# Dilated attention on Trainium2: value projection of two head pairs at a time, with 512 weight columns for each strided stationary piece

## The chip, the cores and the metric

The kernel runs on one core of one Trainium2 chip. The metric is the device time of one execution in microseconds, and the median of the runs is compared. Five engines work beside each other: TensorE (PE, with its weight loads shown apart as PEld), VectorE (DVE), ScalarE (ACT), GpSimd (POOL) and the queue of SyncE (SP), from which this kernel issues its DMAs. An engine works through its own instructions in the order in which the program's scheduler put them, and waits on semaphores for the others.

## The reference, cut to what matters

The whole computation is two transformer blocks on 512 tokens of width 1024. The change touches the first mixer only, the dilated attention. It has three groups (dilations 1, 4 and 16) of eight heads of 128 channels:

```python
def dilated_attention_mixer(x, w_qkv, w_o, rel_bias):
    qkv = (x @ w_qkv).reshape(B, S, N_GROUPS, 3, HEADS_PER_GROUP, HEAD_DIM)
    for g in range(N_GROUPS):
        o, lse = dilated_group_attention(qkv[:, :, g, 0], qkv[:, :, g, 1], qkv[:, :, g, 2],
                                         tbl, WINDOWS[g], DILATIONS[g])
    ...
    alpha = jax.nn.softmax(jnp.stack(lses), axis=0)
    o = jnp.sum(alpha[..., None] * jnp.stack(outs), axis=0)
    return o.reshape(B, S, ATTN_OUT_WIDTH).astype(x.dtype) @ w_o
```

Inside a group with dilation d, tokens are regrouped by their residue modulo d, and each query sees only keys of its own residue. The kernel regroups both dilated groups by residue modulo 4 (four sets of 128 tokens), so that the values of these groups are wanted in the order "residue, then position", one tile of 128 tokens for each residue.

## The kernel before, in words

Products of float32 numbers are made from split numbers: each operand is a high part and a low part, and `mm3` (L159) issues three matmuls on lines L161, L162 and L163: high by high, high by low, low by high. A matmul has a stationary operand, which a weight load (LDWEIGHTS, PEld) brings into the array, and a moving operand that streams past it. Each of the three matmuls has a weight load of its own.

`hT` holds the normalised tokens with channels on the partitions: 2 parts, 8 blocks of 128 channels, 512 tokens. Weights come in tiles of 512 KB: `load` (L138) issues the DMA into a `raw` tile (3 buffers), `cut` (L144) makes the high part on ScalarE (L148) and the low part on VectorE (L149) in a tile `w` (5 buffers). Accumulators are PSUM banks of 512 columns, 6 of them for products (`bank`) and 2 for transposes (`tbank`).

`attn` (L295) works through four head pairs `hp` and three groups `g`. `proj(hp, g)` (L338) is a list of generators that `pipe` runs one after the other, each with its evacuation one round later:

- four jobs `qk`: 128 columns of the queries' or keys' weights are stationary and the 512 tokens move, 24 matmuls for each job;
- two jobs `vp(0)`, `vp(1)` for the values: here 128 tokens are stationary and 256 weight columns (the two heads of the pair) move. A job handles two token tiles, each over 8 channel blocks by 3 matmuls, so `vp(0)` and `vp(1)` make 96 matmuls together. For group 0 the 128 stationary tokens lie side by side; for groups 1 and 2 they are every fourth token, taken from `hT` by this view:

```python
st = [hT[:, i, k].rearrange("p (u r) -> p r u", r=4)[:, t] for i in range(2)]
```

The weights of a value job are two tiles (L355), held through both jobs. One copy on ScalarE (L370) moves each accumulator of a value job to the buffer `V[hp, g]`. Five value buffers (the four tiles of `x`, which is free during this stage, and `vx`) are used in turn.

Beside these lists run the attention steps that `weave` mixes in, from L522 on: beside `proj(hp, 1)` the scores of group 0 and both `pv` of the head pair before; beside `proj(hp, 2)` `to_perm` (which sends softmax statistics through HBM and back in residue order) and the scores of group 1; beside `proj(hp + 1, 0)` the scores of group 2, `combine` (softmax over the groups, with another trip through HBM) and the next bias tile. After the last list come `scores(3, 2)`, `combine(3)` and the output projection, whose first half is woven with the last two `pv`. The order of instructions on each engine is set by the scheduler, which starts from the order in which the generators emit them.

Of the kernel before, what the change touches and what calls it, by code (L numbers as in the profile page):

```python
# [9 lines left out]
F32 = mybir.dt.float32  # L10
# [9 lines left out]
D = 1024  # L20
# [11 lines left out]
def pipe(gens):  # L32
    """software pipeline: each round starts one generator (None: no new one) and advances the ones under way"""
    live = []
    for g in gens:
        if g is not None:
            live.append(g)
        live = [x for x in live if next(x, 0) is None]
        yield
    while live:  # L40
        live = [x for x in live if next(x, 0) is None]
        yield
# [11 lines left out]
def both(*gens):  # L54
    """generators run side by side, as one; a step that ends with "more" goes on after the others' steps"""
    live = list(gens)
    while live:
        r = [next(g, 0) for g in live]
        while "more" in r:
            r = [next(g, 0) if v == "more" else v for g, v in zip(live, r)]  # L60
        live = [g for g, v in zip(live, r) if v is None]
        yield


def woven(*streams):
    """streams of (generator, steps per round), until all end"""
    live = list(streams)
    while live:
        live = [(g, n) for g, n in live if all([next(g, 0) is None for _ in range(n)])]
        yield  # L70
# [11 lines left out]
# order of the first norms (n: a step of a tile's), weights (w) and heads of the bias table (t)  # L82
START = "n0 t0 t0 t0 n0 n1 n0 w0 w1 n1 n2 n2 n1 n3 n2 n3 n3".split()
# mixers of the second block: units of attention by tile and head (d: differential, s: stick-breaking pair,
# m: latent pair), the projections emitted beside them (c, v: by tile; l: weights; u: latent up-projection by tile;
# s: stick-breaking by block), and how many output products follow each further round
# [6 lines left out]
class Net:  # L93
# [31 lines left out]
    def bank(self):  # L125
        """accumulator bank"""
        return self.ps.tile([P, 512], F32, tag="acc", name=self.nm("acc"), bufs=6)

    def tbank(self):
        """bank for transposes"""  # L130
        return self.ps.tile([P, 512], F32, tag="tr", name=self.nm("tr"), bufs=2)

# [1 line left out]
    def weight(self, src, shape, pool=None, tag="w", lo=None):  # L134
        """src: HBM view of shape [128, a, b] with a*b <= 1024, split into hi + lo."""
        return self.cut(self.load(src, shape), shape, pool, tag, lo)
# [15 lines left out]
    def w_in(self, W, c0, width=P):  # L152
        """feature-major weight blocks: [128 k, 8 kb, width]"""
        return self.weight(W[:, c0:c0 + width].rearrange("(k p) c -> p k c", p=P), (W.shape[0] // P, width))
# [10 lines left out]
    def split_to(self, dst, src, hi=None):  # L165
        """dst [P, 2, ...] hi/lo of src (fp32 view in SBUF or PSUM)"""
        self.nc.scalar.copy(dst[:, 0], src)  # L167
        self.nc.vector.tensor_sub(dst[:, 1], src, dst[:, 0].bitcast(F32))  # L168

# [6 lines left out]
    def rsqrt(self, ss, scale, shape, tag):  # L176
        """rsqrt(ss * scale + EPS) on a small fp32 tile"""
# [15 lines left out]
    def rms(self, hs, n=D):  # L193
        """1/rms over the free axis of the two halves hs"""
# [10 lines left out]
    def to_T(self, src, dst, t):  # L205
        """src [P tok, 1024] -> dst[:, hi/lo, kb, t*128..]"""
        nc = self.nc
        for h in range(2):
            b = self.tbank()
            for j in range(4):  # L210
                k = 4 * h + j
                nc.tensor.transpose(b[:, j * P:(j + 1) * P], src[:, k * P:(k + 1) * P], self.ident)  # L212
            bv = b.rearrange("p (k c) -> p k c", k=4)
            self.split_to(dst[:, :, 4 * h:4 * h + 4, t * P:(t + 1) * P], bv)

    def prenorm(self, t, gb, dst=None, src=None, xn=None):
        """steps: the row's rms, the normalised tile (scaled by ScalarE where VectorE is the busier), its transposes"""
# [16 lines left out]
    def postnorm(self, hs, y, t, gb):  # L234
        """x[t] += rmsnorm(hs) * g, by way of y"""
# [7 lines left out]
    def after(self, t, xn=None):  # L243
        """x[t] is final for this sublayer: start the next sublayer's norm, or store"""
# [7 lines left out]
    # feature-major block: psum[128 cols, 512 tok] over all 8 kb  # L252
# [7 lines left out]
    def cols(self, srcs, n, pool, name):  # L260
        """each src (n*128 values, contiguous in HBM) -> tile [128, len(srcs), n], value n*128+p at [p, n]"""
# [13 lines left out]
    def toeplitz(self, table, oh, L, heads, scratch, stage, bank=None):  # L275
        """rows F[h, t] = sum_b table[b, h] * oh[b, t], repeated on 128 rows of HBM scratch [128, heads, L]"""
# [13 lines left out]
    def toeplitz_view(self, scratch, L, h0, nh, c0, n):  # L290
        """[128 i, nh, n]: F[h, c0 + kk - i]"""
        H = scratch.shape[1]
        return hbm(scratch, h0 * L + c0, [[H * L - 1, P], [L, nh], [1, n]])

    def attn(self, l):  # L295
# [4 lines left out]
        with ExitStack() as cx:  # L300
# [26 lines left out]
            nv = 0  # L327
# [10 lines left out]
            def proj(hp, g):  # L338
# [11 lines left out]
                wv = []  # L350

                def vp(tt):
                    nonlocal nv
                    if tt == 0:
                        wv.extend(self.wv0 or [self.w_rows(Wq, 4 * i, 4, base + 2048, 256) for i in range(2)])  # L355
                        self.wv0 = None
                        V[hp, g] = vbuf[nv % 5]
                        nv += 1
                    b = self.bank()
                    for t in (2 * tt, 2 * tt + 1):  # L360
                        for k in range(KD):
                            if g == 0:
                                st = [hT[:, i, k, t * P:(t + 1) * P] for i in range(2)]
                            else:
                                st = [hT[:, i, k].rearrange("p (u r) -> p r u", r=4)[:, t] for i in range(2)]
                            w = wv[k // 4]
                            self.mm3(b[:, (t % 2) * 256:(t % 2) * 256 + 256], st[0], st[1],
                                     w[:, 0, k % 4], w[:, 1, k % 4], k == 0, k == KD - 1)
                    yield
                    nc.scalar.copy(V[hp, g][:, tt * 512:(tt + 1) * 512], b)  # L370
                jobs = [qk(*j) for j in jobs]
                return [vp(0), vp(1)] + jobs if hp == 0 and g == 0 else jobs + [vp(0), vp(1)]

            def start():
                """norms of the four tiles and the first values' weights, in the order of their use"""
# [241 lines left out]
    def exp_small(self, out, x, pool, n):  # L617
        """exp on a small [128, n] fp32 tile, x in [-87, 88] after clamping"""
# [20 lines left out]
    def log_sigmoid(self, x, out, pool, n):  # L639
        """out = min(x, 0) - log1p(exp(-|x|)) on a small [128, n] tile"""  # L640
# [18 lines left out]
    def lru_setup(self, one):  # L659
        """per-channel constants of the recurrent mixer"""  # L660
# [117 lines left out]
    def out_proj(self, W, A, yt, gpost, mid):  # L778
        """yt[t] = (8 k-blocks A) @ W, then x += rmsnorm(yt) * gpost; mid(g) emits g, the first half of K, and
        returns a pool for weights of the second one"""  # L780
# [12 lines left out]
    def setup2(self, pool):  # L793
        """bias rows of the differential attention, masks, rope tables"""
# [15 lines left out]
    def prep(self, l, pool):  # L810
        """what layer l of the second block needs beside its tokens"""
# [45 lines left out]
    def head_rstd(self, src, nh, dh, tag):  # L857
        """1/rms per head of src [P, nh, dh]"""
# [7 lines left out]
    def proj_tok(self, W, c0, width, consume, early=False):  # L866
        """token-major h @ W[:, c0:c0+width]: one generator per token tile, then consume(t, bank)"""
# [19 lines left out]
    def below(self, x, fill=0.0):  # L887
        """fills a [128, 128] block on and above its diagonal"""
# [3 lines left out]
    def exp_rows(self, p, stat, w):  # L892
        """p = exp(p - max), stat [P, 2]: max in, sum out"""
# [4 lines left out]
    def trans_blocks(self, src, n, pool):  # L898
        """transposes of n 128-column blocks of src [P, n*128] -> tile [P, n*128]"""
# [8 lines left out]
    def o_scaled(self, b, nh, dh, c, pool, tag, bufs):  # L908
        """rmsnorm over each head of b * c (c [P, nh] or None) -> token-major tile"""
# [16 lines left out]
    def y_write(self, on, nb, gcol, kb, i):  # L926
        """transposes on [P tok, nb*128], scales by gcol per feature, hi/lo into hT[:, :, kb:kb+nb, tile i]"""
# [10 lines left out]
    def mem_kv(self, l):  # L938
        """keys and values of the memory, a generator"""
# [33 lines left out]
    def mix(self, l):  # L973
        a, nc = self.a, self.nc
        W, Wo = a["w_in_2"][l], a["w_out_2"][l]
        with ExitStack() as cx:
# [64 lines left out]
            # one attention unit = one head (pair) of one query tile  # L1041
# [244 lines left out]
            def gate(*what):  # L1286
                """until all of what is done"""
# [3 lines left out]
            def settle():  # L1291
                """the layer's input back, and the memory attention's buffers"""
# [28 lines left out]
            def paced(g, ns):  # L1321
                """g, by ns steps per round, then by one"""
# [13 lines left out]
    def memory(self, l, x2, b_qz, b_o, b_n, b_g, ons):  # L1336
        """memory attention of one token tile, in buffers of 1024 columns"""
# [82 lines left out]
    def ff_head(self, l):  # L1420
        """first blocks of ffn2(l) for the tokens of the last two tiles, while the first tile is still on its way"""
# [68 lines left out]
    def down_gen(self, W, ks, A, tail):  # L1490
        """token-major partial product over k-blocks ks; tail(t, half, bank) consumes each."""
# [15 lines left out]
    def down_last(self, W, ks, A, tail, post=None, pool=None):  # L1507
        """as down, one token tile after another, each followed by post(t) and the next sublayer's norm"""
# [131 lines left out]
```

## Time and profile before

| | us |
|---|---|
| median of 3 runs | 3063.38 |
| lowest and highest run | 3059.31 and 3063.64 |
| span of the profiled execution, first to last instruction | 3061.5 |
| PE busy in that span | 3012.3 |
| DVE busy | 1669.2 |
| ACT busy | 1254.2 |

The profiled execution has no time of its own beside its span. The span is 1.9 us below the median of the runs, within their spread. The dilated attention takes about the first 612 us; after it come the convolutional feed-forward layers, the recurrent mixer and the second block, which the change does not touch. Matmuls are pipelined: the time that the profile gives one matmul reaches over the start of the next, so what a matmul costs is read from the distance of starts, not from its duration.

### The profile page before, as it was taken

How to read it: one execution, taken by the hardware profiler on the slowest of the kernel's cores; microseconds unless marked ns; L12 is line 12 of the kernel's file. 1: busy time of each engine (PE TensorE's matmuls, PEld its weight loads, DVE VectorE, ACT ScalarE, POOL GpSimd, SP SyncE). 2: the span in 40 equal slices, each digit the busy share in tenths (PEclk: the TensorE clock that was granted, in tenths of full speed). 3: DMA queues.
4: the chain of work that ended last, by engine and by line, in shares of the span. 5: the costliest groups of instructions: out<-in, count | busy, mean ns of one | idle time of the engine just before them, and what ended most of it. 6: DMA issues, size and time to landing. Idle time of an engine off the chain costs nothing.

```text
span 3061.5 us, 37833 instructions
## 1 busy us (share of the span) xinstructions
PE 3012.3 (98%) x14594; PEld 2488.2 (81%) x14594; DVE 1669.2 (55%) x3166; ACT 1254.2 (41%) x2427; POOL 170.5 (6%) x257
## 2 busy tenths in 40 slices
PE   9999999999999999999999999999999999999999
PEld 6889898888888877877787777888887877888887
DVE  3232323364655696644557678754545578754443
ACT  4232322354333575433335467542323457632222
POOL 0000000000000041000001022000000013000000
PEclk9999999999999999999999999999999999999999
DMA  6221222333333323333334332132333333123332
GB/s 185 71 83 56 83 63 76 97 102 92 97 96 91 89 75 112 100 98 107 105 97 138 103 118 84 28 124 84 118 94 111 110 86 104 49 76 91 96 95 70
DMA packets 340023, 287.40 MB, mean 94 GB/s; under 512 B 14041, under 2 KB 280676, under 8 KB 339844
## 3 DMA queue, kind: packets, MB, share of 16 engines
q1 hardware_dynamic: 339844, 284.99, 30.7%
q8 instruction: 115, 1.88, 0.3%
q14 instruction: 64, 0.52, 0.1%
HBM read 272.34 MB, written 12.62 MB: 93 GB/s over the span
## 4 chain that ended last, share of the span: by engine, by line
PE 54%; DVE 6%; ACT 2%; issue 1%; POOL 1%; DMA 1%; POOLq 0%; ACTq 0%; DVEq 0%
PE acc L161 16%; PE acc L163 16%; PE acc L162 16%; PE acc L1048 1%; PE tr L212 1%; PE acc L1061 1%; PE tr L903 1%; DVE w L149 1%; PE acc L1193 1%; PE acc L1387 0%; PE acc L1367 0%; DVE z L1105 0%; DMA raw<-in_w_in_dram 0%; ACT w L148 0%; PE tr L285 0%
## 5 line engine op out<-in xcount | busy, mean ns | idle before, releaser
L149 DVE TENSOR_TENSOR w<-raw,w 128x1024 fp32r<-128x1024 f32 (+1 forms) x456 | 553.9, 1217 | 489.2 <-ACT w L148 488.6
L161 PE MATMUL acc<-hT,w 128*128 128x512 f32 (+1 forms) x1992 | 761.0, 383 | 1.5 <-ACT w L148 1.2
L163 PE MATMUL acc<-hT,w 128*128 128x512 f32 (+1 forms) x1992 | 757.6, 380 | 3.0 <-DVE w L149 2.8
L162 PE MATMUL acc<-hT,w 128*128 128x512 f32 (+1 forms) x1992 | 759.0, 381 | 0.4 <-DVE hT L168 0.4
L148 ACT CAST w<-raw 128x1024 fp32r<-128x1024 f32 (+2 forms) x464 | 477.9, 1033 | 551.5 <-PE acc L163 469.3
L163 PEld LDWEIGHTS acc<-hT,w 128*128 128x128 f32 x1992 | 374.9, 188 | 83.5 <-DVE w L149 4.3
L161 PEld LDWEIGHTS acc<-hT,w 128*128 128x128 f32 x1992 | 374.4, 188 | 82.9 <-issue 2.6
L162 PEld LDWEIGHTS acc<-hT,w 128*128 128x128 f32 x1992 | 374.6, 188 | 78.5 <-DVE hT L168 1.1
L161 PE MATMUL acc<-w,act 128*128 128x512 f32 x896 | 355.1, 397 | 0.8 <-ACT act L167 0.8
L162 PE MATMUL acc<-w,act 128*128 128x512 f32 x896 | 354.3, 396 | 0.0
L163 PE MATMUL acc<-w,act 128*128 128x512 f32 x896 | 352.8, 394 | 0.0
L161 PE MATMUL acc<-w,hT 128*128 128x256 f32 (+2 forms) x896 | 335.1, 374 | 0.8 <-ACT w L148 0.8
L163 PE MATMUL acc<-w,hT 128*128 128x256 f32 (+2 forms) x896 | 326.0, 364 | 0.0
L162 PE MATMUL acc<-w,hT 128*128 128x256 f32 (+2 forms) x896 | 325.1, 363 | 0.0
L562 DVE SCALAR_TENSOR_TENSOR u<-acc,cw,u 128x511 f32<-128x511 f32 x192 | 143.5, 748 | 205.9 <-ACT u L560 202.8
L161 PEld LDWEIGHTS acc<-w,hT 128*128 128x128 f32 x896 | 205.6, 229 | 21.1 <-issue 2.4
L162 PEld LDWEIGHTS acc<-w,hT 128*128 128x128 f32 x896 | 205.8, 230 | 17.1 <-issue 2.4
L163 PEld LDWEIGHTS acc<-w,hT 128*128 128x128 f32 x896 | 205.6, 229 | 15.2
L161 PEld LDWEIGHTS acc<-w,act 128*128 128x128 f32 x896 | 168.3, 188 | 42.6 <-ACT act L167 2.1
L163 PEld LDWEIGHTS acc<-w,act 128*128 128x128 f32 x896 | 168.3, 188 | 41.3 <-DVE act L168 0.6
L162 PEld LDWEIGHTS acc<-w,act 128*128 128x128 f32 x896 | 168.4, 188 | 39.2
L560 ACT ACTIVATE u<-acc,cw 128x512 f32<-128x512 f32 x96 | 74.7, 778 | 219.5 <-PE acc L163 219.3
(376 smaller groups left out, 3307.5 us busy)
## 6 DMA issues: line engine op xcount, KB each, us to landing
raw<-in_w_ff_dram SPq DMA_DIRECT2D x128, 512.0 KB
raw<-in_ffn_w_up_dram SPq DMA_DIRECT2D x96, 512.0 KB
raw<-in_attn_w_qkv_dram SPq DMA_DIRECT2D x72, 512.0 KB
raw<-in_ffn_w_down_dram SPq DMA_DIRECT2D x48, 512.0 KB
raw<-in_w_in_dram SPq DMA_DIRECT2D x40, 512.0 KB
raw<-in_lru_w_in_dram SPq DMA_DIRECT2D x16, 512.0 KB
raw<-in_w_out_dram SPq DMA_DIRECT2D x16, 512.0 KB
x<-in_x_dram SPq DMA_DIRECT2D x8, 512.0 KB
```

The costliest lines, as they stand in the source:

```text
L148: nc.scalar.copy(w[:, 0], raw)
L149: (lo or nc.vector).tensor_sub(w[:, 1], raw, w[:, 0].bitcast(F32))
L161: mm(out, sh, mh, start=first, stop=False)
L162: mm(out, sh, ml, start=False, stop=False)
L163: mm(out, sl, mh, start=False, stop=last)
L212: nc.tensor.transpose(b[:, j * P:(j + 1) * P], src[:, k * P:(k + 1) * P], self.ident)
L560: nc.scalar.activation(u, b, AF.Identity, bias=cw[:, 3, j:j + 1], scale=cw[:, 2, j:j + 1])
L562: nc.vector.scalar_tensor_tensor(u[:, s:], b[:, :S - s], cw[:, i, j:j + 1], u[:, s:], op0=ALU.mult, op1=ALU.add)
L903: nc.tensor.transpose(b[:, j * P:(j + 1) * P], src[:, j * P:(j + 1) * P], self.ident)
L1048: nc.tensor.matmul(o[:, oc:oc + dv], pT[:, k * P:(k + 1) * P], v(k), start=(k == 0), stop=(k == i))
L1061: nc.tensor.matmul(b[:, :w], QZ[:, h, m, i * P:(i + 1) * P], kT[:, h, :w], start=True, stop=True)
L1193: nc.tensor.matmul(b[:, :w], MT[:96, i, 0, h], MT[:96, :i + 1, 1, h], start=True, stop=True)
```

## The change

The queries, the keys, and the values of group 0 are made as before. For the values of the two dilated groups a new job `vpair` takes the place of `vp`: it projects the values of one group for two head pairs at once. A moving operand is 512 weight columns (four heads), so the same stationary piece is loaded once where it was loaded twice, in two different lists. `proj(hp, 1)` now makes the values of group 1 for `hp` and `hp + 1` where `hp` is even, and the values of group 2 for `hp - 1` and `hp` where it is odd, ahead of its query and key jobs; `proj(hp, 2)` makes no values. A job has two accumulators, one for each token tile, with the channel blocks as its outer loop; four weight tiles of 256 rows by 512 columns are held through both jobs. Each accumulator is copied out in two halves, one head pair by ScalarE and one by VectorE. Since some values now live longer, a table gives each its buffer, and two of them take a buffer of the pool `oT`. The diff without comments and blank lines:

```diff
-            nv = 0
+            vhome = {(0, 0): 0, (0, 1): 1, (1, 1): 2, (1, 0): 3, (0, 2): None, (1, 2): 4,
+                     (2, 0): 0, (2, 1): None, (3, 1): 1, (3, 0): 3, (2, 2): 2, (3, 2): 4}
...
                 wv = []
+                vg = 2 if g == 1 and hp % 2 else g
+                def v_home(h):
+                    n = vhome[h, vg]
+                    V[h, vg] = oTs.tile([P, D], F32, tag="oT", name=self.nm("v")) if n is None else vbuf[n]
                 def vp(tt):
-                    nonlocal nv
                     if tt == 0:
                         wv.extend(self.wv0 or [self.w_rows(Wq, 4 * i, 4, base + 2048, 256) for i in range(2)])
                         self.wv0 = None
-                        V[hp, g] = vbuf[nv % 5]
-                        nv += 1
+                        v_home(hp)
                     b = self.bank()
                     for t in (2 * tt, 2 * tt + 1):
                         for k in range(KD):
-                            if g == 0:
-                                st = [hT[:, i, k, t * P:(t + 1) * P] for i in range(2)]
-                            else:
-                                st = [hT[:, i, k].rearrange("p (u r) -> p r u", r=4)[:, t] for i in range(2)]
                             w = wv[k // 4]
-                            self.mm3(b[:, (t % 2) * 256:(t % 2) * 256 + 256], st[0], st[1],
-                                     w[:, 0, k % 4], w[:, 1, k % 4], k == 0, k == KD - 1)
+                            self.mm3(b[:, (t % 2) * 256:(t % 2) * 256 + 256], hT[:, 0, k, t * P:(t + 1) * P],
+                                     hT[:, 1, k, t * P:(t + 1) * P], w[:, 0, k % 4], w[:, 1, k % 4], k == 0, k == KD - 1)
                     yield
                     nc.scalar.copy(V[hp, g][:, tt * 512:(tt + 1) * 512], b)
+                def vpair(tt):
+                    hs = (hp - hp % 2, hp - hp % 2 + 1)
+                    if tt == 0:
+                        c = vg * 3072 + hs[0] * 256 + 2048
+                        wv.extend(self.w_rows(Wq, k, 2, c, 512) for k in range(0, KD, 2))
+                        for h in hs:
+                            v_home(h)
+                    bs = [self.bank(), self.bank()]
+                    for k in range(KD):
+                        w = wv[k // 2]
+                        for b, t in zip(bs, (2 * tt, 2 * tt + 1)):
+                            st = [hT[:, i, k].rearrange("p (u r) -> p r u", r=4)[:, t] for i in range(2)]
+                            self.mm3(b, st[0], st[1], w[:, 0, k % 2], w[:, 1, k % 2], k == 0, k == KD - 1)
+                    yield
+                    for b, t in zip(bs, (2 * tt, 2 * tt + 1)):
+                        nc.scalar.copy(V[hs[0], vg][:, t * 256:(t + 1) * 256], b[:, :256])
+                        nc.vector.tensor_copy(V[hs[1], vg][:, t * 256:(t + 1) * 256], b[:, 256:])
                 jobs = [qk(*j) for j in jobs]
-                return [vp(0), vp(1)] + jobs if hp == 0 and g == 0 else jobs + [vp(0), vp(1)]
+                if g == 0:
+                    return [vp(0), vp(1)] + jobs if hp == 0 else jobs + [vp(0), vp(1)]
+                if g == 1:
+                    return [vpair(0), vpair(1)] + jobs if hp % 2 else jobs + [vpair(0), vpair(1)]
+                return jobs
```

## Rows read from the trace of the kernel before

**Rows 1.** The page's busy times: microseconds, share of the span, instructions.
```profile
PE 3012.3 (98%) x14594; PEld 2488.2 (81%) x14594; DVE 1669.2 (55%) x3166; ACT 1254.2 (41%) x2427; POOL 170.5 (6%) x257
```

**Rows 2.** Busy time by stretch, attention: stretch, length, busy by engine, clock, DMA.
```profile
core 0: us, PE busy (x) PEld busy (x) DVE busy (x) ACT busy (x) POOL busy (x), PEclk, DMA share, GB/s
...
30.00:585.00 555.00, 553.72 (x2701) 487.84 (x2701) 159.88 (x415) 151.30 (x334) 0.00 (x0) 1.00 0.27 80
```

**Rows 3.** Timeline where a strided value pass begins: start, duration, engine, line.
```profile
91.87 0.40 PE L163 MATMUL acc<-hT,w 128*128 128x512 f32 x1
91.87 0.31 PEld L161 LDWEIGHTS acc<-w,hT 128*128 128x128 f32 x1
92.11 0.28 PE L161 MATMUL acc<-w,hT 128*128 128x256 f32 x1
...
92.23 0.39 PE L162 MATMUL acc<-w,hT 128*128 128x256 f32 x1
...
92.46 0.40 PE L163 MATMUL acc<-w,hT 128*128 128x256 f32 x1
```

**Rows 4.** Timeline where the same pass of 96 matmuls ends.
```profile
114.16 0.40 PE L163 MATMUL acc<-w,hT 128*128 128x256 f32 x1
...
114.39 0.39 PE L161 MATMUL acc<-hT,w 128*128 128x512 f32 x1
...
114.62 0.39 PE L162 MATMUL acc<-hT,w 128*128 128x512 f32 x1
```

**Rows 5.** PE's timeline, ends of a contiguous value pass of 96 matmuls.
```profile
185.49 0.28 PE L161 MATMUL acc<-w,hT 128*128 128x256 f32 x1
185.61 0.28 PE L162 MATMUL acc<-w,hT 128*128 128x256 f32 x1
...
196.80 0.40 PE L161 MATMUL acc<-hT,w 128*128 128x512 f32 x1
```

**Rows 6.** Weight loads by form, 92 to 114.2 us (strided): busy, mean ns.
```profile
L163 PEld LDWEIGHTS acc<-w,hT 128*128 128x128 f32 x32 | 10.6, 330 | 0.0
```

**Rows 7.** The same, 185.5 to 196.7 us (contiguous).
```profile
L163 PEld LDWEIGHTS acc<-w,hT 128*128 128x128 f32 x32 | 6.0, 187 | 0.0
```

**Rows 8.** Busy time of work on `w` tiles, first and last of eight strided passes.
```profile
91.99:114.27 22.28, 22.28 (x98) 22.28 (x97) 2.45 (x2) 2.09 (x2) 0.00 (x0) 1.00 0.08 24
...
562.70:585.10 22.40, 22.40 (x98) 22.40 (x96) 2.45 (x2) 2.09 (x2) 0.00 (x0) 1.00 0.07 25
```

**Rows 9.** ScalarE's groups by form, 0 to 640 us.
```profile
L148 ACT CAST w<-raw 128x1024 fp32r<-128x1024 f32 x83 | 86.8, 1047 | 177.4 <-PE acc L163 134.9 <-issue 38.2 <-DMA raw<-in_attn_w_qkv_dram 2.8
...
L370 ACT COPY x<-acc 128x512 f32<-128x512 f32 x20 | 11.8, 588 | 92.5 <-PE acc L163 92.5
...
L286 ACT COPY fz<-tr 128x255 f32<-128x255 f32 x16 | 5.5, 373 | 11.2 <-DMA tz<-fz 5.8 <-PE tr L285 5.2
```

**Rows 10.** VectorE's groups by form, 0 to 640 us.
```profile
L149 DVE TENSOR_TENSOR w<-raw,w 128x1024 fp32r<-128x1024 f32 x83 | 101.4, 1223 | 216.4 <-ACT w L148 216.4
...
L433 DVE CUSTOM_DVE_ANT_0 p<-acc,bi 128x256 f32<-128x256 f32 x24 | 9.1, 418 | 0.0
```

**Rows 11.** The DMA queue's waits, 0 to 620 us: total, times, longest.
```profile
SPq L141 <- DVE w L149: 370.3, 60, 22.9
```

**Rows 12.** VectorE's busy time while it reduces both heads' scores of group 0.
```profile
203.20:207.60 4.40, 4.04 (x19) 1.00 0.27 79
```

**Rows 13.** PE's waits, 30 to 612 us: total, times, longest.
```profile
PE acc L507 <- ACT pT L500: 1.7, 4, 0.5
```

**Rows 14.** Timeline of the DMA queue, return of the last statistics.
```profile
546.16 0.37 SPq L450 DMA_DIRECT2D st<-sd  x1
```

**Rows 15.** VectorE's timeline, first reader of these statistics.
```profile
559.52 0.16 DVE L459 TENSOR_TENSOR M<-st 128x8 f32<-128x8 f32 x1
```

**Rows 16.** PE's timeline after the last value pass.
```profile
585.14 1.95 PE L428 MATMUL acc<-k,q 128*128 128x128 f32 x16
586.84 0.47 PE L161 MATMUL acc<-w,oT 128*128 128x512 f32 x1
...
597.24 0.22 PE L473 MATMUL tr<-ident,wr 8*128 8x8 f32 x1
```

## The prediction

> **What bounds the kernel now.** I read the page first. PE is busy for 3012.3 of 3061.5 us, VectorE for 55% of the span and ScalarE for 41% [rows 1]. That does not yet say that PE limits the stage in question, so I read the busy times by stretch next. From 30 to 585 us, the dilated attention without its start, PE is busy for 553.72 of 555.00 us at a granted clock of 1.00 (the 2.4 GHz level), VectorE for 159.88 and ScalarE for 151.30 [rows 2]. PE is never empty here, and the others have two thirds of their time free: a microsecond taken from PE's queue in this stage is a microsecond off the end, as long as nothing begins to keep PE waiting.
>
> Busy does not mean at its best, so the third view is the timeline of single matmuls. I take distances of starts. In the query and key jobs (512 moving columns, contiguous stationary operand) one matmul follows the other by 0.23 us [rows 4]. In the strided value pass (256 columns) the distance is also 0.23 us [rows 3]. The first 512-column matmul after the pass starts at 114.39, the last one before it at 91.87: 22.52 us for 97 intervals [rows 3, 4]. The contiguous value pass, also with 256 columns, needs 196.80 - 185.49 = 11.31 us for its 96 matmuls, 0.118 us each [rows 5]. So half as many columns take half the time with contiguous tokens and no less time with every fourth token. The loads differ too: a strided one lasts 330 ns, a contiguous one 187 ns [rows 6, 7]. The strided pass is bound by its weight loads, and the columns that could stream beside them are missing.
>
> **What is removed.** Groups 1 and 2 have 4 head pairs x 2 groups x 96 = 768 strided matmuls of 256 columns. An interval costs (22.52 - 0.118) / 96 = 0.2333 us (the 0.118 is the short stream of the last one), so they take 768 x 0.2333 = 179.2 us of PE's queue. The busy times confirm the size: 22.3 to 22.4 us for each of the passes that lie in one piece [rows 8] (five of the eight; the other three have `pv` mixed in).
>
> **What takes their place.** 384 strided matmuls of 512 columns. No row shows this operation in a series, so I bound it. From below: the stream alone, 0.2333 us, as in the query and key jobs [rows 4]. From above: a load of 0.2333 us that makes no progress while a stream runs, 0.4667 us, which would give no gain. Where between them? Four readings decide. First, in the contiguous pass the period is 0.118 us and half a 512-column interval is 0.117, so there a load costs next to nothing beside its stream [rows 5]: loads do run under streams. Second, a matmul in the strided series lasts 0.40 us where an unhindered one lasts 0.28 [rows 3, 5]: it leaves the queue when the stream before has ended and waits 0.12 us more for its load. 0.12 us of stream plus 0.12 us of waiting is the load's 0.233. Third, a strided load behind a 512-column matmul does occur, once at the start of a pass: the load begins with that matmul at 91.87, and the next matmul begins 0.24 us later [rows 3]. Fourth, if load and stream added up inside the 0.233 us, the 97 intervals of a pass would be 0.233 (the 512-column stream ahead) + 96 x 0.233 = 22.63 us, where the rows give 22.52 [rows 3, 4]; if the load starts with the stream before it, they are 96 x 0.233 + 0.118 = 22.52. I take 0.235 us, close to the lower bound and a little over it because load and stream now both need their whole period: 384 x 0.235 = 90.2 us. Gain on PE: 179.2 - 90.2 = 89.0 us.
>
> The Trainium skill, page "TensorE: Matmul & The Clock Gate", section "Part 3: Packing small matmuls — row/col tiling", says that a weight load overlaps a matmul in flight only when it goes to another row group of the array; all matmuls here use all 128 rows. By that rule load and stream add up, and the gain would be the 42 us of the first rival below instead of the 86 us of the sum. The trace speaks against it, by the contiguous pass and by the length of the strided one.
>
> **What moves.** The pass in `proj(hp, 1)` keeps its 96 matmuls at the same interval; the whole gain comes out of the four `proj(hp, 2)`, 22.4 us each, which keep only four query and key jobs (96 intervals, 22.4 us) and their scores.
>
> - Weights: 16 tiles before (8 passes x 2), 16 after (4 x 4), with the same bytes, casts (1.05 us on ScalarE) and subtractions (1.22 us on VectorE) [rows 9, 10]. They come closer together, one per 5.6 us in place of 11.2 in the value jobs, which is the pace of the query and key jobs. Today the casts wait mostly for PE to free a buffer (134.9 us) and only 2.8 us for a DMA [rows 9], and the DMA queue waits 370.3 us for `raw` tiles to come free [rows 11]: supply runs ahead. `vpair` holds 4 of 5 `w` buffers. The next list's first weight has the fifth. Its second weight waits for the first tile that the second `vpair` is done with, 12 matmuls or 2.8 us into it, then needs 1.05 + 1.22 us; PE asks for it 8.4 + 5.6 = 14.0 us after that release. Margin 11.7 us: no cost. Were the cover gone, each late microsecond would be PE's.
> - Evacuation: 16 copies of 588 ns on ScalarE become 16 there and 16 on VectorE of half the width, each between 373 ns (a 255-column copy) and 418 ns (a 256-column operation from PSUM) [rows 9, 10]. One behind the other that is 0.8 us for a bank; hidden by the next job's 5.6 us of matmuls.
> - Banks: a `vpair` takes two of six. In the two odd lists `vpair(0)` meets four banks of the scores of group 0 in the same round, so `vpair(1)` needs two of them back. VectorE needs 4.04 us for those scores' reductions and one subtraction [rows 12]; the price lies between 0 and 5 us in each of two lists. I take 1 us each.
> - `pv` in the odd lists: the last value jobs no longer cover the last `pv` steps, query and key jobs do. PE's waits there are 1.7 us in total today [rows 13]; I add 1 us.
> - Shorter `proj(hp, 2)`: `to_perm`'s return is issued at 546.16 and its first reader runs at 559.52 [rows 14, 15], so the trip takes at most 13.4 us; the list still has 22.4. No cost.
> - The tail: `scores(3, 2)` now follows directly on the last key job instead of on a value pass. `combine`'s trip stays covered by the output projection, 586.84 to 597.24 [rows 16]. The second half of the keys must still be copied out (one VectorE copy); 0 to 1 us, taken as 0.
>
> **Sum.** 89.0 - 3 = 86 us less: the span of 3061.5 us becomes 2975.5. The median of the runs stands 1.9 us above that span: 2977 us.
>
> **The rivals.**
>
> 1. *Load and stream add up.* Then the period is 0.117 + 0.233 = 0.35 us, the new matmuls take 134.4 us, the gain is 179.2 - 134.4 - 3 = 42 us: 3021 us. For it: no series of this kind exists in the trace, and the recorded starts of weight loads in the strided series trail each stream. Against it: the contiguous pass and the 22.52 us of the strided one. Chance 0.06.
> 2. *Part is given back* by banks, `pv` or the new order of the queues: the upper prices above (5 us in each odd list, 1 us at the tail) and as much again for `pv`, 12 to 30 us: 2988 to 3004 us. For it: in the odd lists values, scores and `pv` now meet in the first rounds. Against it: PE has other jobs ready in every round. Chance 0.09.
> 3. *The change does not do what it says*: the 512-column matmul with strided tokens needs 0.46 us, because a load stands still under a stream. No gain, 3063 us. The contiguous pass speaks against it. Chance 0.02.
> 4. *Slower: the `w` buffers starve PE.* With four of five held, the second job's weight of the next list would have to be 11.7 us late to cost anything, and 11.7 + 22.4 = 34 us late after each of the four passes to eat the 89 us. For it: only one buffer is left in those 14 us. Against it: the queue's waits, which show supply ahead of use. From 34 us on it decides; at 36 us late the time is 3063 + 4 x 2 = 3071 us. Chance 0.02.
>
> **How the numbers follow.** My forecast, 2967 to 2988, has the remaining 0.81. Its lower end is the gain at the lower bound (89.6) with nothing given back, 2974, less the runs' spread of 4 us and the 3 us for which other waits in the stage may shrink. The range of 2966 to 2996 takes in that and about half of the second rival. A change of 0.2%, 6 us, is about what this measurement can tell from none. Faster than that: 0.81 + 0.06 + 0.09 = 0.96; within it 0.02; slower 0.02.
>
> **What would show it.** In the profile after, the 512-column matmuls with `w` moving and `hT` stationary should rise by 128 on each of L161 to L163's successors and the 256-column ones fall by 256; a strided series should show starts 0.233 to 0.24 us apart, and its matmuls should last about 0.40 us as the 512-column ones do now. The stretch from 30 us to the end of attention should be 86 us shorter with PE still busy for all but some 4 us. Starts 0.35 us apart would prove the first rival; gaps on PE with `w` as their releaser the fourth; gaps released by VectorE's or ScalarE's copies the second. A gain that comes from elsewhere, or matmuls 0.235 apart with a gain below 75 us, would make the reasoning wrong.

## The result, and the profile after

The changed kernel takes 2976.91 us (median of 4 runs, 2974.8 to 2979.35) where the kernel before takes 3062.62 us beside it: a ratio of 0.9724, 95% interval 0.971 to 0.9738. The forecast was 2977 us in a range of 2966 to 2996. The profiled execution took 2979.35 us, 1.75 us more than its span of 2977.6 us.

The page of the kernel after, busy times, answers to [rows 1]; the busy time by stretch answers to [rows 2]:

```profile
PE 2927.2 (98%) x14210; PEld 2402.7 (81%) x14210; DVE 1676.8 (56%) x3182; ACT 1250.8 (42%) x2427; POOL 169.3 (6%) x257
```

```profile
30.00:500.00 470.00, 467.34 (x2319) 401.13 (x2318) 166.08 (x430) 149.00 (x335) 0.00 (x0) 1.00 0.32 96
```

PE has 384 matmuls less and 85 us less of busy time; VectorE has the 16 new copies. In the attention PE is still almost never empty: it is idle for 2.7 us of 470, against 1.3 of 555 before.

The timeline where the first strided pass begins, to be read against [rows 3] (start, duration, engine, line):

```profile
92.33 0.40 PE L163 MATMUL acc<-hT,w 128*128 128x512 f32 x1
92.34 0.31 PEld L161 LDWEIGHTS acc<-w,hT 128*128 128x128 f32 x1
92.57 0.40 PE L161 MATMUL acc<-w,hT 128*128 128x512 f32 x1
92.58 0.31 PEld L162 LDWEIGHTS acc<-w,hT 128*128 128x128 f32 x1
...
92.81 0.40 PE L162 MATMUL acc<-w,hT 128*128 128x512 f32 x1
```

And PE's timeline where it ends, against [rows 4]:

```profile
115.36 0.40 PE L163 MATMUL acc<-w,hT 128*128 128x512 f32 x1
115.59 0.39 PE L161 MATMUL acc<-hT,w 128*128 128x512 f32 x1
```

Before, the second strided matmul was recorded 0.12 us after the first and then lasted 0.39 to 0.40 us, waiting for its load. Now the starts are evenly spaced from the first one on, and a matmul lasts as long as an unhindered one of 512 columns: the load has found its cover. From 92.57 to 115.36 there are 95 intervals, 0.2399 us each.

The weight loads by form inside this pass, against [rows 6], and PE's waits from 30 to 530 us, against [rows 13]:

```profile
L162 PEld LDWEIGHTS acc<-w,hT 128*128 128x128 f32 x32 | 10.0, 312 | 0.0
```

```profile
PE acc L532 <- ACT pT L525: 3.2, 4, 1.1
```

The only wait of a product on PE that grew is that of `pv` (L507 before, L532 after) for a transposed probability tile that ScalarE copies, from 1.7 to 3.2 us. No wait for `w` and none for a copy of the values appears in this list. The copies of the values may still have a part in it: ahead of the longest wait, which ends at 203.93 us, ScalarE makes two of them (0.37 us each) and the high part of a weight tile (1.05 us) between 201.36 and 203.39 us, and only then copies the probability tile. Which of these costs the time was not separated.

The end of the attention is read at the first `postnorm` (L241, tile `yt`): the line's own view gives, for the kernel before and then for the kernel after, times of the first and last of four:

```profile
L241 DVE SCALAR_TENSOR_TENSOR x<-yt,ss,x x4: 1272/1275/1284, 629.2 to 650.7; 128x1024 f32<-128x1024 f32 x4
```

```profile
L241 DVE SCALAR_TENSOR_TENSOR x<-yt,ss,x x4: 1275/1278/1285, 544.8 to 566.3; 128x1024 f32<-128x1024 f32 x4
```

That is 84.4 us earlier; the two spans differ by 83.9. The whole gain lies in the attention; all that comes behind it takes together 0.5 us longer.

### The profile page after: what moved, and what is told of

Same layout as the page of the kernel before. It is cut to its first block, busy times and chain, and to the rows that moved or that the text cites. A ratio compares the mean times of both kernels' runs of the same rounds, so it can differ in the third digit from the quotient of the medians.

```text
span 2977.6 us, 37084 instructions
## 1 busy us (share of the span) xinstructions
PE 2927.2 (98%) x14210; PEld 2402.7 (81%) x14210; DVE 1676.8 (56%) x3182; ACT 1250.8 (42%) x2427; POOL 169.3 (6%) x257
## 4 chain that ended last, share of the span: by engine, by line
PE 55%; DVE 7%; ACT 2%; issue 1%; POOL 1%; DMA 1%; POOLq 0%; ACTq 0%; DVEq 0%
PE acc L161 16%; PE acc L162 16%; PE acc L163 16%; PE acc L1073 1%; PE tr L212 1%; PE acc L1086 1%; DMA raw<-in_w_in_dram 1%; PE tr L928 1%; DVE w L149 1%; PE acc L1218 1%; PE acc L1412 0%; ACT w L148 0%; PE acc L1392 0%; DVE z L1130 0%; DVE lru_hs L773 0%
## 5 line engine op out<-in xcount | busy, mean ns | idle before, releaser
L161 PE MATMUL acc<-w,hT 128*128 128x512 f32 (+2 forms) x768 | 286.2, 373 | 1.3 <-ACT w L148 1.3
L163 PE MATMUL acc<-w,hT 128*128 128x512 f32 (+2 forms) x768 | 276.2, 360 | 0.0
L162 PE MATMUL acc<-w,hT 128*128 128x512 f32 (+2 forms) x768 | 275.2, 358 | 0.0
L161 PEld LDWEIGHTS acc<-w,hT 128*128 128x128 f32 x768 | 161.4, 210 | 21.4 <-issue 2.4
L162 PEld LDWEIGHTS acc<-w,hT 128*128 128x128 f32 x768 | 161.7, 211 | 17.1 <-issue 2.4
L163 PEld LDWEIGHTS acc<-w,hT 128*128 128x128 f32 x768 | 161.3, 210 | 15.1
```

Source lines behind the costliest of these rows:

```text
L161: mm(out, sh, mh, start=first, stop=False)
L162: mm(out, sh, ml, start=False, stop=False)
L163: mm(out, sl, mh, start=False, stop=last)
```

## The experiments

Ten kernels were run beside the kernel before. Times are medians; the ratio is to the kernel before on the same chip.

**1. The stride alone.** The kernel before with contiguous tokens as the stationary piece of all value matmuls.

```diff
-  st = [hT[:, i, k].rearrange("p (u r) -> p r u", r=4)[:, t] for i in range(2)]
+  st = [hT[:, i, k, t * P:(t + 1) * P] for i in range(2)]
```

> The kernel before, but the value matmuls of groups 1 and 2 take 128 tokens that lie side by side as their stationary piece, so these values belong to other tokens than the attention wants; all counts and shapes stay. Load theory (the strided weight load of 0.233 us bounds the pass, a contiguous one hides under 256 columns): starts 0.118 us apart, 768 x (0.2333 - 0.118) = 88.5 us less, 2974 us. Rival (256 columns are too few for whatever reason, or the order of the lists costs the time): starts stay 0.233 us apart, 3063 us.

Measured: 2974.2 us, ratio 0.9711 (0.9696 to 0.9725). PE's timeline of this kernel, first two matmuls of group 1's pass and the one that follows the pass:

```profile
92.21 0.28 PE L161 MATMUL acc<-w,hT 128*128 128x256 f32 x1
92.33 0.28 PE L162 MATMUL acc<-w,hT 128*128 128x256 f32 x1
...
103.52 0.40 PE L161 MATMUL acc<-hT,w 128*128 128x512 f32 x1
```

96 matmuls in 11.31 us, as in [rows 5]. With the same counts, shapes, weight tiles and order of the lists, the view of the tokens alone was worth 88 us, in a kernel that leaves the right tokens out.

**2. The new order without the wider stream.** The kernel after, each 512-column matmul cut in two.

```diff
-  for k in range(KD):
-      ...
-              self.mm3(b, st[0], st[1], w[:, 0, k % 2], w[:, 1, k % 2], k == 0, k == KD - 1)
+  for c in (slice(0, 256), slice(256, 512)):
+      for k in range(KD):
+          ...
+                  self.mm3(b[:, c], st[0], st[1], w[:, 0, k % 2, c], w[:, 1, k % 2, c], k == 0, k == KD - 1)
```

> The kernel after, same lists, buffers, weight tiles and copies, but every 512-column value matmul is cut into two of 256 columns with a strided load of its own each: 768 loads as before, in the new order of the lists. Load theory: starts 0.233 us apart, 768 x 0.2333 = 179.2 in place of 384 x 0.2398 = 92.1 us, so 87 us are lost again: 3064 us, or the time of before plus the 1 to 3 us that the new order gives back. Rival (the gain came from moving the values between the lists, or from other weight tiles): the time stays near 2977 us.

Measured: 3061.37 us, ratio 0.9996 (0.9987 to 1.0006). PE's timeline inside a pass:

```profile
99.73 0.40 PE L161 MATMUL acc<-w,hT 128*128 128x256 f32 x1
99.97 0.40 PE L162 MATMUL acc<-w,hT 128*128 128x256 f32 x1
100.20 0.40 PE L163 MATMUL acc<-w,hT 128*128 128x256 f32 x1
```

The starts are 0.23 us apart again and the gain is gone. Lists, buffers, weight tiles and split copies are worth nothing by themselves. They also cost nothing here: PE's waits for `pv` are 1.7 us, as before.

**3. A shorter stream in the kernel before.** 128 of the 256 columns.

```diff
+  n = 128 if g else 256
-  self.mm3(b[:, (t % 2) * 256:(t % 2) * 256 + 256], st[0], st[1],
-           w[:, 0, k % 4], w[:, 1, k % 4], k == 0, k == KD - 1)
+  self.mm3(b[:, (t % 2) * 256:(t % 2) * 256 + n], st[0], st[1],
+           w[:, 0, k % 4, :n], w[:, 1, k % 4, :n], k == 0, k == KD - 1)
...
```

> The kernel before, but the value matmuls of groups 1 and 2 stream 128 of their 256 columns; the values of the pair's second head are left out and those of the first stand in both places. Load theory (interval is the longer of load and stream): the 0.233 us stay, 3063 us within 3. Rival (load and stream add up in part, 0.117 us of stream and 0.117 of uncovered load): the interval falls by half the stream, 0.058 us, 768 times: 3018 us.

Measured: 3079.32 us, ratio 1.0055 (1.004 to 1.007): neither. The timeline of this kernel inside a pass, PE alone:

```profile
92.28 0.39 PE L162 MATMUL acc<-w,hT 128*128 128x128 f32 x1
...
92.52 0.39 PE L163 MATMUL acc<-w,hT 128*128 128x128 f32 x1
...
92.75 0.39 PE L161 MATMUL acc<-w,hT 128*128 128x128 f32 x1
```

The interval stayed at 0.23 us, as the load theory says and the rival does not. What made the kernel slower is in another column, PEclk, of the busy time by stretch, and in PE's timeline at the end of the pass and behind it:

```profile
31.00:70.00 39.00, 39.00 (x158) 27.84 (x157) 9.10 (x12) 11.92 (x22) 0.00 (x0) 1.00 0.46 141
...
99.00:113.70 14.70, 14.70 (x65) 14.70 (x65) 1.23 (x1) 1.69 (x3) 0.00 (x0) 0.50 0.01 1
```

```profile
113.29 0.43 PE L162 MATMUL acc<-w,hT 128*128 128x128 f32 x1
113.52 0.43 PE L163 MATMUL acc<-w,hT 128*128 128x128 f32 x1
...
114.29 0.63 PE L162 MATMUL acc<-hT,w 128*128 128x512 f32 x1
114.72 0.63 PE L163 MATMUL acc<-hT,w 128*128 128x512 f32 x1
115.14 0.63 PE L161 MATMUL acc<-hT,w 128*128 128x512 f32 x1
```

While PE streamed 128 columns per strided load, its granted clock fell to 0.50, the 1.2 GHz level, with the pass's own starts still 0.23 us apart, and the query and key jobs behind the pass began at that level, with starts 0.42 us apart instead of 0.23. The first `postnorm` comes at 645.8 us, 16.6 us later than before, and the whole time is 17 us longer: the attention holds all of it. Both kernels issue the same matmuls in the same order, so their distances of starts can be compared one by one up to the end of the attention: 165 of them, outside the passes and at the lower clock, are 18.4 us longer than before, and all the others together are 1.8 us shorter. So the time is lost where the clock is low, and nowhere else. The edit also splits ScalarE's copy of each of these accumulators in two, which the lines above leave out; PE's waits stay at 1.7 us in total. No run separated the shorter stream from these copies as the reason why the clock fell.

**4. Every second token.** The same kernel before, with a step of two.

```diff
-  st = [hT[:, i, k].rearrange("p (u r) -> p r u", r=4)[:, t] for i in range(2)]
+  st = [hT[:, i, k].rearrange("p (u r) -> p r u", r=2)[:, t % 2, (t // 2) * P:(t // 2 + 1) * P] for i in range(2)]
```

> The kernel before, but the stationary piece is every second token in place of every fourth, so the values of groups 1 and 2 belong to other tokens than the attention wants. Theory A (any stride makes the load slow): 0.233 us, 3063 us. Theory B (the load's time grows with the reach of the piece, 0.118 at one, 0.233 at four): between, about 0.16 us and 3005 us. Theory C (two neighbours in 16 bytes are fetched together, so every second token is still free): 0.118 us and 2974 us. The Trainium skill, page SBUF — State Buffer, section Port Architecture, speaks for C where it says that full bandwidth needs two hits per 16-byte line.

Measured: 2976.92 us, ratio 0.9721 (0.9706 to 0.9735). PE's timeline, the last matmul ahead of a pass, its first, and the one that follows its 96; then the loads by form inside it:

```profile
127.22 0.39 PE L163 MATMUL acc<-hT,w 128*128 128x512 f32 x1
127.45 0.28 PE L161 MATMUL acc<-w,hT 128*128 128x256 f32 x1
...
138.96 0.40 PE L161 MATMUL acc<-hT,w 128*128 128x512 f32 x1
```

```profile
L162 PEld LDWEIGHTS acc<-w,hT 128*128 128x128 f32 x29 | 5.7, 198 | 0.0
```

0.120 us for each: theory C. The Trainium skill's sentence on 16-byte lines, in the page "SBUF — State Buffer", stands in its section "Door 1: The DMA port swizzle (why `[64,N]` ≈ `[32,N]`)"; the section's name in the expectation above is wrong. The runs agree with its demand for two hits in a line: with two tokens of 4 bytes in 16 the interval is 0.120 us, with one it is 0.233. The sentence behind it in the Trainium skill gives 4 fp32 as how far one can stride for free; here a step of four is the one that costs, and the measurement decides. That lines of 16 bytes are the reason is the account of the Trainium skill; the runs by themselves show that the limit lies above a step of 8 bytes and not above one of 16, and no step of three was run.

**5. Every eighth element.**

```diff
-  st = [hT[:, i, k].rearrange("p (u r) -> p r u", r=4)[:, t] for i in range(2)]
+  st = [hT[:, i, k - k % 2:k - k % 2 + 2].rearrange("p k s -> p (k s)").rearrange("p (u r) -> p r u", r=8)[:, t + 4 * (k % 2)] for i in range(2)]
```

> The kernel before, but the stationary piece of the value matmuls of groups 1 and 2 is every eighth element of two neighbouring channel blocks, so these values are sums over other numbers than the attention wants; counts and shapes stay. Theory A (from a step of 16 bytes on every element is a fetch of its own, and more cannot be lost): starts stay 0.233 us apart, 3062 us. Theory B (the load's time grows with the reach, 0.118 at one, 0.120 at two, 0.233 at four): about 0.46 us, 768 x 0.23 = 177 us more, 3240 us.

Measured: 3067.41 us in a single run beside 3062.96. PE's timeline, and the loads by form:

```profile
93.64 0.40 PE L161 MATMUL acc<-w,hT 128*128 128x256 f32 x1
93.88 0.40 PE L162 MATMUL acc<-w,hT 128*128 128x256 f32 x1
94.12 0.41 PE L163 MATMUL acc<-w,hT 128*128 128x256 f32 x1
```

```profile
L161 PEld LDWEIGHTS acc<-w,hT 128*128 128x128 f32 x31 | 10.5, 338 | 0.0
```

The interval is 0.240 us, by which 768 matmuls take 5 us more than at 0.2333. The first `postnorm` comes at 635.5 us, 6.3 us later than before; the two single times differ by 4.5 us. Theory B is refuted: from a step of four to a step of eight the interval hardly grows. That it is paid once per element, as theory A has it, fits these four steps but is not shown by itself.

**6. What is left of the load beside 512 columns.** The kernel after with contiguous tokens in `vpair` (the edit of the first experiment).

> The kernel after, but with 128 neighbouring tokens as the stationary piece of the paired value matmuls, so the values of groups 1 and 2 belong to other tokens than the attention wants. What is left of the load's cost beside 512 columns: theory A (the strided load still adds the 0.0065 us by which the interval of 0.2398 exceeds the contiguous 0.2333): 384 x 0.0065 = 2.5 us less than the changed kernel, 2974.5 us, starts 0.233 us apart. Theory B (the 0.0065 us come from the two alternating accumulators or the moving weights, not from the stride): starts stay 0.240 us apart and the time 2977 us.

Measured: 2971.77 us, ratio 0.9703 (0.9689 to 0.9716), beside 2976.2 us, 0.9716 (0.9703 to 0.973), for the changed kernel in the same series. PE's timeline:

```profile
92.54 0.40 PE L161 MATMUL acc<-w,hT 128*128 128x512 f32 x1
...
114.31 0.39 PE L163 MATMUL acc<-w,hT 128*128 128x512 f32 x1
```

95 intervals of 0.2292 us, even shorter than the 0.233 of the query and key jobs. By this measure the strided load still adds 0.0107 us to each matmul, 384 x 0.0107 = 4.1 us, and the medians differ by 4.4. Theory A, with a larger size than expected.

**7. 384 columns.** The kernel after with a shorter stream.

```diff
-  self.mm3(b, st[0], st[1], w[:, 0, k % 2], w[:, 1, k % 2], k == 0, k == KD - 1)
+  self.mm3(b[:, :384], st[0], st[1], w[:, 0, k % 2, :384], w[:, 1, k % 2, :384], k == 0, k == KD - 1)
...
-  nc.vector.tensor_copy(V[hs[1], vg][:, t * 256:(t + 1) * 256], b[:, 256:])
+  nc.vector.tensor_copy(V[hs[1], vg][:, t * 256:(t + 1) * 256], b[:, 128:384])
```

> The kernel after, streaming 384 of the 512 columns of each paired value matmul; the values of the last head of the four are left out and its neighbour's stand in their place. Load theory (interval is the longer of load and stream): the load's 0.233 us stay, 384 x 0.0065 = 2.5 us less than the changed kernel, 2974.5 us. Rival (at 512 columns the stream sets the interval, and a shorter stream shortens it): 0.175 to 0.18 us, 384 x 0.06 = 23 us less, 2954 us.

Measured: 2970.44 us, ratio 0.97 (0.9687 to 0.9713). PE's timeline:

```profile
93.22 0.40 PE L161 MATMUL acc<-w,hT 128*128 128x384 f32 x1
93.45 0.40 PE L162 MATMUL acc<-w,hT 128*128 128x384 f32 x1
93.69 0.40 PE L163 MATMUL acc<-w,hT 128*128 128x384 f32 x1
```

The interval is 0.232 to 0.233 us with 128, 256 and 384 columns, and 0.240 with 512. Its own 384 x 0.007 = 2.7 us explain half of the 5.8 us; another 1.5 us are PE's waits for `pv`, which fell from 3.2 to 1.7 us. Another 0.5 us lie ahead of the first pass, where the edit has done nothing yet: its first matmul starts at 91.88 us, in the run of experiment 10 at 92.38. The last 1.1 us are within the spread of the runs.

**8. The place of group 2's values.** The kernel after, with these values at the end of `proj(hp, 2)` of the even pairs.

```diff
-  vg = 2 if g == 1 and hp % 2 else g
+  vg = g
...
-  if g == 1:
-      return [vpair(0), vpair(1)] + jobs if hp % 2 else jobs + [vpair(0), vpair(1)]
-  return jobs
+  return jobs if hp % 2 else jobs + [vpair(0), vpair(1)]
```

> The kernel after, with the paired values of group 2 made at the end of proj(hp, 2) of the even head pairs, with the values of group 1 one list earlier, and none in the odd lists; same matmuls, buffers and counts. Theory A (what the change gave back, some 2 us, is values, scores and pv meeting in the odd lists): PE's waits for pv go back below 2 us, 2975 us. Theory B (pv loses cover when a list has only four jobs beside it): PE's waits grow beyond the 3.2 us of the changed kernel, 2977 to 2982 us.

Measured: 2978.93 us, ratio 0.9727 (0.9714 to 0.974), against 0.9716 (0.9703 to 0.973) for the changed kernel: unclear. PE's waits for `pv` are 2.8 us in six places where the changed kernel has 3.2 in four. Neither theory is borne out; the place of these values does not matter by an amount that these runs can tell.

**9. Four weight buffers.**

```diff
-  self.ws = pool("ws", 5)
+  self.ws = pool("ws", 4)
```

> The kernel after with 4 buffers for weight tiles in place of 5, in every stage. In the attention the paired value jobs then hold all of them. Supply theory (the next list's first weight gets its buffer 2.8 us into the second job, needs 2.3 us, and is wanted 8.4 us after that release, so 6.1 us of margin are left): the first postnorm of the attention comes at 545 us within 1, as in the changed kernel, and PE has no waits for w between 30 and 530 us. Rival (the held buffers are at their limit): waits for w appear on PE, at least 2 us in each of the four passes, and the attention ends 8 us later or more. What the later stages lose with 4 buffers is not asked.

Measured, by the line's own view of `postnorm`:

```profile
L241 DVE SCALAR_TENSOR_TENSOR x<-yt,ss,x x4: 1275/1278/1285, 544.8 to 566.4; 128x1024 f32<-128x1024 f32 x4
```

The attention ends at the same 544.8 us as with five buffers, and PE waits for `w` nowhere in it. The whole kernel took 3003.47 us in a single run, and its span of 3001.8 us is 24.2 us longer than the changed kernel's. With the attention unchanged, these 24.2 us lie in later stages.

**10. The changed kernel again**, beside experiments 6 to 8.

> The changed kernel unaltered, to stand beside the next three on the same chip: 2977 us within 2.

Measured: 2976.2 us (2973.17 to 2978.37).

## Why the prediction was right

**The bound.** The prediction took PE's queue in the attention as the end of everything and the strided load as the bound of the value pass. Experiment 1 shows the second part by itself: with the view of the tokens as the only edit, the passes fall from 0.233 to 0.118 us for each matmul and the time by 88 us. The first part is shown by the sum: PE's busy time fell by 85.1 us and the span by 83.9.

**The interval with 512 columns** was the choice on which the size rested, between 0.2333 and 0.4667 us. The prediction took 0.235; the trace shows 0.2399. The term is mis-sized by 384 x 0.005 = 1.9 us; the mechanism, the longer of load and stream, held. Experiments 3 and 7 and [rows 3] show the flat part of it (0.232 to 0.233 us at 128, 256 and 384 columns), experiment 6 the stream's part (0.229, so that the lower bound of 0.2333 us for the stream alone was a little too high for this place). At 512 columns, where both are nearly equal, the interval lies 0.007 us above the load's and 0.011 us above the stream's. Why is open; the two alternating accumulators alone are not the reason, since they cost nothing at 384 columns.

The four readings behind this choice are not of one worth. The fourth sets 22.52 us against an interval that was itself worked out from these 22.52 us by assuming the outcome, so as it stands it proves nothing. The starts inside the pass give the interval by themselves: 92.46 to 114.16 are 93 intervals of 0.2333 us [rows 3, 4], and with that the reading holds. The third, the only strided load behind a 512-column matmul that was looked at, gave 0.24 us, nearer to the outcome than the 0.235 taken.

**The first rival**, load and stream in series, is refuted: it asked for 0.35 us. So is the third, which asked for 0.46. With the first falls, for this kernel, the rule of the Trainium skill's page "TensorE: Matmul & The Clock Gate", section "Part 3: Packing small matmuls — row/col tiling", that a load overlaps a matmul only in another row group: here they share all rows, and a strided load that takes 0.233 us by itself fits, with 512 columns of stream, into 0.240 us. (Another sentence of that section of the Trainium skill also lets a load go ahead into a background weight buffer; the runs do not speak against that one.)

**What the change gives back.** The prediction allowed 3 us: 2 for banks and 1 for `pv`. The account on the trace: a pass that is removed took 22.52 us and leaves one interval of 0.23, so four of them free 89.1 us; a pass that stays grew from 22.52 to 115.59 - 92.33 = 23.26 us, four times 0.74 = 3.0 us. That is 86.2, and 84.4 were measured. Of the 1.8 us between, 1.5 are the grown waits of `pv`, half a microsecond more than allowed; 0.46 lie ahead of the first pass (its first matmul starts at 92.57 instead of 92.11), where the change has done nothing yet and where the other kernels have it between 91.44 and 92.54. The two make 0.2 us more than the gap, about what such an account can resolve. Banks cost nothing: no wait of PE for a copy of scores or values appears. So the prediction took 1.9 us too little for the matmuls, left out 0.9 us at the ends of the passes (89.0 - 1.9 = 87.1 against 86.2), and allowed 1.2 us too much for what is given back. This leaves its 86 us 1.6 above the 84.4 of the trace. That the median of 2976.91 us meets the forecast to 0.1 us is luck: the four runs alone spread over 4.6 us.

**Supply of weights**, the rival on the other side, had a margin of 11.7 us by the prediction's sum. Experiment 9 takes a whole buffer away and the attention does not move, which bears the margin out.

**The new order** costs nothing and earns nothing by itself (experiment 2). Of the 12 to 30 us of the second rival 1.5 us of waits appeared, and the same order has none of them in experiments 2 and 7; experiment 8 could not tell one place of group 2's values from the other.

No kernel that computes all of the reference beat the changed one. What is left to gain from the strided load in these passes is bounded by experiment 6: 4.4 us, if it cost nothing at all.

## What to carry to other kernels

When matmuls of different widths start at the same distance, the stream is not what is being paid: compare the distance of starts, and the duration of the weight loads, between two places with the same shape but different views of the stationary operand. In these runs the interval was the longer of load and stream, to within 0.011 us. So a slow load is cured either by streaming more columns for each piece, as here, or by a view whose neighbours lie at most 8 bytes apart; both were worth 85 to 88 us of 3062. The second was run only with the wrong tokens: what it would cost to lay the tokens in that order was not measured. Before filling the gap, ask what else the wider job holds (weight buffers, banks) and for how long; here the margins were large enough.

## What the runs showed of the hardware

- The load time of a 128-column fp32 piece had two levels at the four steps that were run, not a slope: 187 ns recorded contiguous and 198 ns with every second element, 330 ns with every fourth and 338 ns with every eighth. The starts beside them were 0.118, 0.120, 0.233 and 0.240 us apart with 256 columns, so the first two loads may need less than that.
- A PE that the profile shows as busy all the time fell to half its clock when only 128 columns streamed for each strided load (granted clock 0.50 from 99 to 113.7 us in experiment 3). The interval of the strided loads stayed 0.23 us on both sides of that fall, while that of the 512-column matmuls behind the pass went from 0.23 to 0.42 us: the load does not follow this clock, the streams do.
- Contiguous 512-column matmuls followed each other by 0.2292 us in experiment 6 and by 0.233 us in the query and key jobs. The two differ in which operand is the weights and in alternating between two accumulators; no run separated these.
